# Moving three PSUM tiles of a recurrence: scores and gate product to the other pool, turned sample rows into the outputs' bank

## The chip, the core and the metric

The kernel runs on one core of a Trainium2 chip. The metric is the device time of one execution in microseconds (us), given as the median of several runs. The profile is of one execution of its own. The engines go by short names: PE is TensorE (matrix products), DVE is VectorE, ACT is ScalarE, POOL is GpSimd, SP is SyncE. PSUM is the memory that PE writes its products to and that the other engines read; it is handed out in banks, and every tile of 128 x 512 float32 here is one bank.

## What is computed

One layer of a decoder step for 256 prompt rows and 8 x 8 sample rows (T = 320 columns in the kernel, the first TP = 256 of them the prompt): norm, one wide projection, three branches, an output projection and a gated feed-forward part. The change lies in the first branch, a recurrence over tokens with a 64 x 64 state for each of 12 heads:

```python
def _wkv7_step(S, inp):
    r, w, k, v, kk, a = inp
    sa = jnp.einsum('bhvk,bhk->bhv', S, -kk)
    S = S * w[:, :, None, :] + sa[..., None] * (kk * a)[:, :, None, :] + v[..., None] * k[:, :, None, :]
    return S, jnp.einsum('bhvk,bhk->bhv', S, r)
...
    s_fin, o = lax.scan(_wkv7_step, s0.astype(f32), xs)
    o = jnp.swapaxes(o, 0, 1)
    mean = jnp.mean(o, axis=-1, keepdims=True)
    var = jnp.mean(jnp.square(o - mean), axis=-1, keepdims=True)
    o = (o - mean) * lax.rsqrt(var + RW_GN_EPS)
    o = o.reshape(b, t, RW_WIDTH) * prm['ln_x_w'].astype(f32) + prm['ln_x_b'].astype(f32)
    bonus = jnp.sum(r * k * prm['r_k'].astype(f32), axis=-1, keepdims=True) * v
    o = (o + bonus.reshape(b, t, RW_WIDTH)) * g.astype(f32)
```

The prompt starts from a state of zeros; the sample rows start from eight given states, one for each group of eight rows.

## The kernel before

**Fill.** All large projections are a queue of jobs. A step of a job multiplies a 128 x 128 piece of weights with 320 columns; the product is made of three passes (lines 102 to 104), of the weights' high and low part (`wh`, `wl`) with the activations' high and low part. ScalarE rounds a loaded piece to `wh` (line 374) and VectorE subtracts for `wl` (line 375), a few pieces ahead. While the recurrence runs, these jobs fill PE between its steps.

**The recurrence** takes the heads in six pairs, called pairs 1 to 6 here. For each pair three generators run: `early` (lines 509 to 631), `inverse` (633 to 675) and `late` (677 to 797). A program-building loop (`pump`) advances a clock by a constant for every step of fill and resumes a generator when the time that its last `yield` gave is over or its condition holds. So the order of PE's instructions is the order in which the code is run: PE's order is written by hand (`MANUAL` holds PE alone), and PE takes it strictly in that order. The other engines' order comes from a scheduler, which places instructions by estimates of its own; when the program is built, a changed dependency can move instructions on VectorE, ScalarE and GpSimd too.

**What one pair does, in order.** `early`: two small products for decay and rate (lines 513 to 515); element-wise work on VectorE that ends with `ar` (line 555); the scores, 20 small products in chunks of 32 rows, chunks 0 to 7 into `ps1` and 8 to 9 into `ps2` (lines 566 and 571 to 574), which VectorE masks into `BT` (line 569); the masked scores go through DRAM (lines 579 and 582) into `NI`; transposes of `bk`, `ar` and `sv` (lines 589, 595). `inverse`: a triangular inverse of `NI` by many small VectorE operations (lines 643 to 663), then the result `R` goes back through DRAM (line 666) to `IT` (line 671, four DMAs). `late`: a solve with `IT`; in the bank `pso` the product of the samples' states (line 714), which opens the bank; ScalarE copies a part of it to `Wu` (line 716). Then the carry products of the prompt's chunks (line 724), in two groups with a bank each, out of which VectorE adds `AB` and a new `ar` (lines 727 and 730); the state products into `psb` (line 734); `Wu` turned into `psu` by four products with the identity (line 739), which VectorE adds in two halves to rows of `AU` (line 743); 16 products into `pso` for the prompt's outputs (line 749); then seven hops from state to state (line 753) with fill in between; and last the rest of the outputs into `pso` (lines 758 to 765), the new sample states `pss`, the output norm, and the gate's product `psg` (line 793), which VectorE multiplies in (line 795).

**Banks.** The small tiles share two pools of two banks each, `pea` and `pch`, in which a new tile takes the bank of the tile before last and must wait until that one has been read. Before the change everything in `early` and everything from the output norm on takes from `pea`; `late` takes from `pch` through the helper `bank()`: two tiles of the solve, two of the carry, `psu`, `pss`. So `psu` gets the bank of the first group of the carry. `pso` and `psb` have a pool of one bank each, and `pso` uses columns 0 to 255 for outputs of the prompt, TP = 256 to 319 for outputs of the samples and 320 to 383 for what becomes `Wu`.

Of the kernel before, what the change touches and what calls it, by code (L numbers as in the profile page):

```python
# [9 lines left out]
F32 = mybir.dt.float32  # L10
# [6 lines left out]
T = 320  # L17
TP = 256
# [45 lines left out]
def tile_hybrid_step(ctx: ExitStack, tc: tile.TileContext, i, o):  # L64
    nc = tc.nc
    V, A, G, PE = nc.vector, nc.scalar, nc.gpsimd, nc.tensor
# [9 lines left out]
    C = {n: cst[:, s] for n, s in COFF.items()}  # L76
# [65 lines left out]
    def spread(psum, ex, nh, tbs=TB):  # L142
        ps = psum.tile([128, 512], F32, tag="sm", name="sm")
        n = 0
        for j, (_, c0, c1) in enumerate(tbs):
            lhs = ex[:, j:j + 1].to_broadcast([128, 128]) if nh == 1 else ex[:, j, :]
            PE.matmul(ps[:, n:n + c1 - c0], lhs, C["ident"][:, c0:c1], start=True, stop=True)  # L147
            n += c1 - c0
        return ps[:, :n]
# [19 lines left out]
    with tc.tile_pool(name="st", bufs=1, side="right") as st, tc.tile_pool(name="st2", bufs=3, side="right") as st2, \  # L169
# [136 lines left out]
        sm = spread(smp, smt, 1, tbs=TB[:2])  # L306
# [121 lines left out]
    with tc.tile_pool(name="rws", bufs=1, side="right") as rws, tc.tile_pool(name="rwp", bufs=2, side="right") as rwp, \  # L428
# [29 lines left out]
        Wu = rws.tile([128, TS], F32, name="Wu")  # L458
# [50 lines left out]
        def early(hp):  # L509
# [49 lines left out]
            AU = rwm.tile([128, 10, 128], F32, tag="AU", name="AU")  # L559
            AP = rwm.tile([128, 5, 128], F32, tag="AP", name="AP")  # L560
            fss = [slice(64 * h, 64 * h + 64) for h in range(2)]

            def scores(pv, lo, hi):
                for c in range(lo, hi):
                    for fs in fss:
                        PE.matmul(pv[fs, c - lo, :].rearrange("p (x t) -> p x t", x=2), bk[fs, c, :], ar[fs, :, 32 * c:32 * c + 32], start=True, stop=True)
# [1 line left out]
            def masked(pv, lo, hi, mask):  # L568
                V.tensor_mul(out=BT[:, lo:hi, 64:128], in0=pv, in1=C[mask].unsqueeze(1).to_broadcast([128, hi - lo, 64]))

            ps1 = pea.tile([128, 512], F32, tag="sm", name="sm").rearrange("p (c t) -> p c t", t=64)
            ps2 = pea.tile([128, 512], F32, tag="sm", name="sm").rearrange("p (c t) -> p c t", t=64)
            scores(ps1, 0, 8)
            scores(ps2, 8, 10)
            masked(ps1, 0, 8, "tmask")
# [10 lines left out]
            ps1 = pea.tile([128, 512], F32, tag="sm", name="sm")  # L586
            ps2 = pea.tile([128, 512], F32, tag="sm", name="sm")
# [23 lines left out]
            ps1 = pea.tile([128, 512], F32, tag="sm", name="sm")  # L611
# [7 lines left out]
            ps1 = pea.tile([128, 512], F32, tag="sm", name="sm").rearrange("p (c t) -> p c t", t=64)  # L619
# [8 lines left out]
            bonus = rwm.tile([128, T], F32, tag="bonus", name="bonus")  # L628
            V.tensor_mul(out=bonus, in0=psb, in1=sv)
            spawn(late(hp, ar, pc, bonus, BT, it, AU, AP))  # L630
            state["early"] = hp + 1

# [44 lines left out]
        def late(hp, ar, pc, bonus, BT, it, AU, AP):  # L677
# [6 lines left out]
            fss = [slice(64 * h, 64 * h + 64) for h in range(2)]  # L684
            uss = [slice(64 * h, 64 * h + 32) for h in range(2)]

            def bank():
                return pch.tile([128, 512], F32, tag="sm", name="sm")
# [12 lines left out]
            ps1, ps2 = bank(), bank()  # L701
# [8 lines left out]
            pso = psop.tile([128, 512], F32, tag="acc", name="pso")  # L710
            psw = pso[:, TP:TP + 128].rearrange("p (x t) -> p x t", x=2)
            for b in range(8):
                for fs in fss:
                    PE.matmul(psw[fs, :, 8 * b:8 * b + 8], S0[fs, b, :], ar[fs, :, TP + 8 * b:TP + 8 * b + 8],
                              start=b == 0, stop=False, skip_group_check=True)
            A.copy(out=Wu, in_=psw[:, 1, :])
            yield SLV
            for lo, hi in ((1, 5), (5, 8)):
# [6 lines left out]
                for h in range(2):  # L725
                    hs = slice(64 * h, 64 * h + 64)
                    V.tensor_add(out=AB[hs, lo - 1:lo - 1 + n, hs], in0=pv[hs, 0:n, 0:64],
                                 in1=C["ident"][hs, hs].unsqueeze(1).to_broadcast([64, n, 64]))
# [3 lines left out]
            for c in range(8):  # L732
                for h in range(2):
                    PE.matmul(psb[fss[h], 64 * c:64 * c + 64], BT[fss[h], c, 0:64], AU[fss[h], c, 64:128],
                              start=c == 0, stop=c == 7, skip_group_check=True)
            psu = bank()
            for cc in range(2):
                for h in range(2):
                    PE.matmul(psu[uss[h], 64 * cc:64 * cc + 64], Wu[fss[h], 32 * cc:32 * cc + 32], C["ident"][fss[h], fss[h]], start=True, stop=True)
            SA = rw1.tile([128, 8, 64], F32, tag="SA", name="SA")  # L740
            A.activation(out=SA[:, 0, :], in_=psb[:, 0:64], func=AF.Copy, scale=pc[:, 0:1])
            for h in range(2):
                V.tensor_add(out=AU[uss[h], 8:10, 64:128], in0=psu[uss[h], 0:128].rearrange("p (c v) -> p c v", v=64), in1=AU[uss[h], 8:10, 64:128])
            UVm = rw1.tile([128, 512], F32, tag="UVm", name="UVm").rearrange("p (c s v) -> p c s v", s=4, v=64)
            G.tensor_mul(out=UVm, in0=AU[:, 8:10, 64:128].unsqueeze(2).to_broadcast([128, 2, 4, 64]),
                         in1=C["smask"].unsqueeze(1).unsqueeze(3).to_broadcast([128, 2, 4, 64]))
            for c in range(8):
                for h in range(2):
                    PE.matmul(pso[fss[h], 32 * c:32 * c + 32], AU[fss[h], c, 64:128], BT[fss[h], c, 64:96],
                              start=False, stop=False, skip_group_check=True)  # L750
            yield HOP
            for c in range(1, 8):
                PE.matmul(psb[:, 64 * c:64 * c + 64], AB[:, c - 1, :], SA[:, c - 1, :], start=False, stop=True,
                          skip_group_check=True)
# [3 lines left out]
            for c in range(1, 8):  # L758
                for h in range(2):
                    PE.matmul(pso[fss[h], 32 * c:32 * c + 32], SA[fss[h], c - 1, :], ar[fss[h], 0, 32 * c:32 * c + 32],  # L760
                              start=False, stop=False, skip_group_check=True)
            for c in range(8, 10):
                for h in range(2):
                    PE.matmul(pso[fss[h], 32 * c:32 * c + 32], AU[fss[h], c, 64:128], BT[fss[h], c, 64:96],
                              start=False, stop=c == 9, skip_group_check=True)
# [23 lines left out]
            V.tensor_mul(out=ob, in0=ob, in1=rn)  # L789
            A.activation(out=ob, in_=ob, func=AF.Identity, scale=col("lnw", hp), bias=col("lnb", hp))  # L790
            yield 2.0
            psg = pea.tile([128, 512], F32, tag="sm", name="sm")[:, :T]
            PE.matmul(psg, lw[:, 1, cs], lora[1], start=True, stop=True)
            V.tensor_add(out=ob, in0=ob, in1=bonus)
            V.tensor_mul(out=ob, in0=psg, in1=ob)
# [3 lines left out]
        def allearly():  # L799
            for hp in range(6):  # L800
                yield from early(hp)
# [284 lines left out]
    with tc.tile_pool(name="mg", bufs=1, side="right") as mg, tc.tile_pool(name="mg2", bufs=2, side="right") as mg2, \  # L1086
# [76 lines left out]
        for k in range(16):  # L1163
            for half in range(2):
                for j in range(4):
                    h, l = wc[k // 8 * 4 + j]
# [15 lines left out]
    with tc.tile_pool(name="ff", bufs=1, side="left") as ff, tc.tile_pool(name="fft", bufs=2, side="left") as fft, \  # L1182
# [7 lines left out]
        for g, gn in enumerate((8, 8, 8, 8, 8, 4)):  # L1190
            fs = []
            for jj in range(gn):
# [7 lines left out]
                             in1=S2[:, TP:T].rearrange("p (b t) -> p b t", t=8))  # L1200
                for e in range(2):
                    G.tensor_copy(out=cout[:, j, :, e], in_=zp[:, 256 + e:337 + e:10])  # L1202
                c = fft.tile([128, 336], F32, tag="cv", name="cv")
# [9 lines left out]
                             in1=c[:, 256:336].rearrange("p (b t) -> p b t", t=10)[:, :, 2:10])  # L1213
# [27 lines left out]
        with tc.manual_schedule(engines=MANUAL):  # L1241
            for q, sq_ in enumerate((facc, sq)):
                for j, (t0, _, _) in enumerate(TB):
                    PE.matmul(pst[:, j:j + 1], sq_[:, t0:t0 + 128], C["ones"][:, 0:1], start=q + j == 0, stop=q == 1,  # L1244
                              skip_group_check=True)
                for _ in range(7):
                    PE.matmul(wps, fs[1][0][:, 0:128], fs[0][0], start=True, stop=True)  # L1247
        v = fft.tile([128, 8], F32, tag="rsv", name="rsv")[:, :3]
# [4 lines left out]
        with tc.tile_pool(name="pt", bufs=3, space=PSUM) as ptp:  # L1253
            sy = spread(smp, r, 1)
            A.copy(out=SY, in_=sy)
            for m, n, en in TAIL:
# [6 lines left out]
                t = ptp.tile([128, 2, 512], F32, tag="t", name="pt")[:, :n, :T]  # L1263
# [138 lines left out]
```

## Time and profile before

| quantity | value |
|---|---|
| median of the runs | 2039.72 us (2036.27, 2039.72, 2040.2) |
| the profiled execution | 2036.6 us |
| its span, first to last instruction | 2034.8 us |
| granted TensorE clock, mean over the span | 0.988 |
| busy share of the span: PE, DVE, ACT, POOL | 97%, 60%, 41%, 10% |
| PE's longest wait by line: line 739 for line 730 of VectorE | 17.6 us in 5 waits |

The profile is read in four steps: the busy times say which engine bounds the kernel; the list of waits says what that engine waited for, line by line; the timeline of one place says who came when, with idle time in square brackets ahead of the instruction that ended it and the instruction that released it; and the table by stretches says at which clock TensorE ran there (1.00 is 2.4 GHz, 0.50 is 1.2 GHz).

### The profile page before, as it was taken

How to read it: one execution, taken by the hardware profiler on the slowest of the kernel's cores; microseconds unless marked ns; L12 is line 12 of the kernel's file. 1: busy time of each engine (PE TensorE's matmuls, PEld its weight loads, DVE VectorE, ACT ScalarE, POOL GpSimd, SP SyncE). 2: the span in 40 equal slices, each digit the busy share in tenths (PEclk: the TensorE clock that was granted, in tenths of full speed). 3: DMA queues.
4: the chain of work that ended last, by engine and by line, in shares of the span. 5: the costliest groups of instructions: out<-in, count | busy, mean ns of one | idle time of the engine just before them, and what ended most of it. 6: DMA issues, size and time to landing. Idle time of an engine off the chain costs nothing.

```text
span 2034.8 us, 36379 instructions
## 1 busy us (share of the span) xinstructions
PE 1981.6 (97%) x14888; PEld 1928.4 (95%) x14888; DVE 1215.6 (60%) x2019; ACT 829.2 (41%) x1353; POOL 195.7 (10%) x446
## 2 busy tenths in 40 slices
PE   8999898899999999999999999999999999999997
PEld 8888898889998999999999999999999999999997
DVE  7788868874467754444447653554555555555456
ACT  5544344333444433333444433333343333343335
POOL 4412122211200000000100100000000000000001
PEclk9999899999999999999999999999999999999999
DMA  7543343333645444544552444454444444444433
GB/s 277 174 140 120 95 134 102 101 103 128 203 169 160 136 130 153 160 152 150 194 187 91 155 145 153 148 179 161 150 151 147 154 146 155 146 155 146 151 135 127
DMA packets 89688, 303.28 MB, mean 149 GB/s; under 512 B 11500, under 2 KB 13190, under 8 KB 89504
## 3 DMA queue, kind: packets, MB, share of 16 engines
q1 hardware_dynamic: 79920, 273.42, 40.1%
q0 software_dynamic: 8880, 26.71, 3.9%
q8 instruction: 117, 1.92, 0.4%
q10 hardware_dynamic: 720, 0.82, 0.1%
q14 instruction: 51, 0.42, 0.1%
HBM read 293.53 MB, written 9.34 MB: 149 GB/s over the span
## 4 chain that ended last, share of the span: by engine, by line
PE 57%; issue 5%; POOL 1%; DVE 0%; ACT 0%; POOLq 0%; DVEq 0%
PE bigps L102 18%; PE bigps L103 18%; PE bigps L104 18%; PE bigps L1171 0%; PE bigps L1169 0%; PE bigps L1172 0%; POOL merged L1094 0%; POOL yacc L1259 0%; POOL yacc L1260 0%; DVE MG L845 0%; PE sm L147 0%; POOL rsr L1119 0%; PE sm L1244 0%; PE sm L1112 0%; PE sm L1247 0%
## 5 line engine op out<-in xcount | busy, mean ns | idle before, releaser
L102 PE MATMUL bigps<-XH,wh 128*128 128x320 f32 x2656 | 843.7, 318 | 0.9 <-ACT gt L862 0.8
L104 PE MATMUL bigps<-XH,wl 128*128 128x320 f32 x2656 | 824.0, 310 | 1.4 <-DVE wl L375 1.3
L103 PE MATMUL bigps<-XL,wh 128*128 128x320 f32 x2656 | 823.7, 310 | 0.0
L98 DVE TENSOR_TENSOR wl<-raw,wh 128x1024 fp32r<-128x1024 f32 (+1 forms) x299 | 357.5, 1195 | 275.3 <-ACT wh L97 274.7
L97 ACT CAST wh<-raw 128x1024 fp32r<-128x1024 f32 (+1 forms) x299 | 306.5, 1025 | 521.5 <-PE bigps L103 412.8
L102 PEld LDWEIGHTS bigps<-XH,wh 128*128 128x128 f32 x2656 | 501.6, 189 | 14.1 <-issue 8.6
L103 PEld LDWEIGHTS bigps<-XL,wh 128*128 128x128 f32 x2656 | 501.9, 189 | 2.2 <-issue 0.2
L104 PEld LDWEIGHTS bigps<-XH,wl 128*128 128x128 f32 x2656 | 501.3, 189 | 2.4 <-DVE wl L375 2.4
L375 DVE TENSOR_TENSOR wl<-raw,wh 128x1024 fp32r<-128x1024 f32 (+2 forms) x212 | 243.2, 1151 | 184.5 <-ACT wh L374 182.0
L374 ACT CAST wh<-raw 128x1024 fp32r<-128x1024 f32 (+2 forms) x212 | 208.4, 984 | 313.0 <-PE bigps L103 250.9
L103 PE MATMUL bigps<-fl,wh 128*128 128x320 f32 x704 | 217.5, 309 | 0.0
L102 PE MATMUL bigps<-fh,wh 128*128 128x320 f32 x704 | 217.4, 309 | 0.0
L104 PE MATMUL bigps<-fh,wl 128*128 128x320 f32 x704 | 217.4, 309 | 0.0
L102 PEld LDWEIGHTS bigps<-fh,wh 128*128 128x128 f32 x704 | 132.2, 188 | 0.2 <-ACT fh L152 0.2
L103 PEld LDWEIGHTS bigps<-fl,wh 128*128 128x128 f32 x704 | 132.2, 188 | 0.1
L104 PEld LDWEIGHTS bigps<-fh,wl 128*128 128x128 f32 x704 | 132.2, 188 | 0.0
L1228 DVE TENSOR_TENSOR yacc<-yacc,bigps 128x320 f32<-128x320 f32 x80 | 38.9, 487 | 84.4 <-PE bigps L104 84.4
L1202 POOL COPY cout<-zp 128x9 f32<-128x9 f32 x88 | 15.5, 206 | 734.0 <-DVE zp L1199 734.0
L102 PE MATMUL bigps<-MG,wh 128*128 128x320 f32 x208 | 64.4, 309 | 0.3 <-ACT MG L844 0.3
L103 PE MATMUL bigps<-MG,wh 128*128 128x320 f32 x208 | 64.3, 309 | 0.0
L104 PE MATMUL bigps<-MG,wl 128*128 128x320 f32 x208 | 64.3, 309 | 0.0
L1198 DVE TENSOR_TENSOR zp<-bigps,S 128x256 f32<-128x256 f32 x44 | 18.7, 425 | 57.0 <-PE bigps L104 57.0
(407 smaller groups left out, 2358.4 us busy)
## 6 DMA issues: line engine op xcount, KB each, us to landing
raw<-in_wup SPq DMA_DIRECT2D x176, 512.0 KB, 3.5
raw<-in_win SPq DMA_DIRECT2D x164, 512.0 KB, 3.6
raw<-in_wdn SPq DMA_DIRECT2D x80, 512.0 KB, 3.2
raw<-in_wo SPq DMA_DIRECT2D x32, 512.0 KB, 3.7
raw<-in_wbr_rw SPq DMA_DIRECT2D x16, 384.0 KB, 3.2
raw<-in_wbr_sw SPq DMA_DIRECT2D x16, 384.0 KB, 3.1
ck<-in_cmk POOLq DMA_DIRECT2D x8, 512.0 KB, 5.1
cv<-in_cmv POOLq DMA_DIRECT2D x8, 512.0 KB, 4.2
```

Of the source, the lines that this page charges most:

```text
L97: A.copy(out=h, in_=raw)
L98: V.tensor_sub(out=l, in0=raw, in1=h.bitcast(F32))
L102: PE.matmul(ps, h, xh, start=start, stop=False)
L103: PE.matmul(ps, h, xl, start=False, stop=False)
L104: PE.matmul(ps, l, xh, start=False, stop=stop)
L374: A.copy(out=h, in_=c[2])
L375: V.tensor_sub(out=l, in0=c[2], in1=h.bitcast(F32))
L1198: V.tensor_mul(out=zp[:, 2:258], in0=psz[:, 0:TP], in1=S2[:, 0:TP])
L1202: G.tensor_copy(out=cout[:, j, :, e], in_=zp[:, 256 + e:337 + e:10])
L1228: V.tensor_add(out=yacc[:, m, :], in0=yacc[:, m, :], in1=ps)
```

## The change

Three tiles get another place in PSUM. The computation is the same.

- The two tiles of the scores (`ps1`, `ps2`) come from `pch` instead of `pea`.
- The gate's product `psg` comes from `pch` (through `bank()`) instead of `pea`.
- `psu`, the turned sample rows, no longer gets a bank of its own from `bank()`. It lies in columns TP + 128 to TP + 255 of `pso` (384 to 511), which nothing used. Since the bank was opened by line 714, its products go without the start flag.

```diff
--- before.py
+++ after.py
@@ -568,8 +568,8 @@
             def masked(pv, lo, hi, mask):
                 V.tensor_mul(out=BT[:, lo:hi, 64:128], in0=pv, in1=C[mask].unsqueeze(1).to_broadcast([128, hi - lo, 64]))
 
-            ps1 = pea.tile([128, 512], F32, tag="sm", name="sm").rearrange("p (c t) -> p c t", t=64)
-            ps2 = pea.tile([128, 512], F32, tag="sm", name="sm").rearrange("p (c t) -> p c t", t=64)
+            ps1 = pch.tile([128, 512], F32, tag="sm", name="sm").rearrange("p (c t) -> p c t", t=64)
+            ps2 = pch.tile([128, 512], F32, tag="sm", name="sm").rearrange("p (c t) -> p c t", t=64)
             scores(ps1, 0, 8)
             scores(ps2, 8, 10)
             masked(ps1, 0, 8, "tmask")
@@ -733,14 +733,15 @@
                 for h in range(2):
                     PE.matmul(psb[fss[h], 64 * c:64 * c + 64], BT[fss[h], c, 0:64], AU[fss[h], c, 64:128],
                               start=c == 0, stop=c == 7, skip_group_check=True)
-            psu = bank()
+            psu = pso[:, TP + 128:TP + 256]
             for cc in range(2):
                 for h in range(2):
-                    PE.matmul(psu[uss[h], 64 * cc:64 * cc + 64], Wu[fss[h], 32 * cc:32 * cc + 32], C["ident"][fss[h], fss[h]], start=True, stop=True)
+                    PE.matmul(psu[uss[h], 64 * cc:64 * cc + 64], Wu[fss[h], 32 * cc:32 * cc + 32], C["ident"][fss[h], fss[h]],
+                              start=False, stop=True, skip_group_check=True)
             SA = rw1.tile([128, 8, 64], F32, tag="SA", name="SA")
             A.activation(out=SA[:, 0, :], in_=psb[:, 0:64], func=AF.Copy, scale=pc[:, 0:1])
             for h in range(2):
-                V.tensor_add(out=AU[uss[h], 8:10, 64:128], in0=psu[uss[h], 0:128].rearrange("p (c v) -> p c v", v=64), in1=AU[uss[h], 8:10, 64:128])
+                V.tensor_add(out=AU[uss[h], 8:10, 64:128], in0=psu[uss[h], :].rearrange("p (c v) -> p c v", v=64), in1=AU[uss[h], 8:10, 64:128])
             UVm = rw1.tile([128, 512], F32, tag="UVm", name="UVm").rearrange("p (c s v) -> p c s v", s=4, v=64)
             G.tensor_mul(out=UVm, in0=AU[:, 8:10, 64:128].unsqueeze(2).to_broadcast([128, 2, 4, 64]),
                          in1=C["smask"].unsqueeze(1).unsqueeze(3).to_broadcast([128, 2, 4, 64]))
@@ -789,7 +790,7 @@
             V.tensor_mul(out=ob, in0=ob, in1=rn)
             A.activation(out=ob, in_=ob, func=AF.Identity, scale=col("lnw", hp), bias=col("lnb", hp))
             yield 2.0
-            psg = pea.tile([128, 512], F32, tag="sm", name="sm")[:, :T]
+            psg = bank()[:, :T]
             PE.matmul(psg, lw[:, 1, cs], lora[1], start=True, stop=True)
             V.tensor_add(out=ob, in0=ob, in1=bonus)
             V.tensor_mul(out=ob, in0=psg, in1=ob)
```

Lines from 740 on are one further down in the changed kernel: line 743 becomes 744, 749 becomes 750, 793 becomes 794, 795 becomes 796.

On PE, in pair 1, from the second group of the carry products (into the bank `sm`) to the end of the outputs' products into `pso`; in brackets the engines whose counts an instruction waits for. Before:

```order
L724 MATMUL sm<-BT,AU 64x96 [waits PE_49]
L724 MATMUL sm<-BT,AU 64x96 x5
L734 MATMUL psb<-AU,BT 64x64 x16
L739 MATMUL sm<-cst,Wu 32x64 [waits DVE_49,PE_49,Activation_49]
L739 MATMUL sm<-cst,Wu 32x64 x3
L749 MATMUL pso<-BT,AU 64x32 x16
```

After:

```order
L724 MATMUL sm<-BT,AU 64x96 [waits PE_49]
L724 MATMUL sm<-BT,AU 64x96 x5
L734 MATMUL psb<-AU,BT 64x64 x16
L739 MATMUL pso<-cst,Wu 32x64 [waits Activation_49]
L739 MATMUL pso<-cst,Wu 32x64 x3
L750 MATMUL pso<-BT,AU 64x32 [waits DVE_49]
L750 MATMUL pso<-BT,AU 64x32 x15
```

The order of the products is the same; the wait on VectorE moved from line 739 to the first product of line 750, and the count that it waits for is the one that the second addition of line 744 brings. The other five pairs read the same way.

On GpSimd, behind the end of pair 1 (`S` are the sample states, `sc` the tile in DRAM between lines 666 and 671, `rsr` a reciprocal root of the output norm, `pc` decay factors for the next pair but one; the numbers count tiles). Before:

```order
L773 DMA out_wkvs<-S_1389 128x512
L666 DMA sc_2523<-R 120x192
L474 COPY shout<-pad 128x9
L681 DMA S_2208<-in_wkv 128x512
L469 MEMSET pad 128x1
L470 COPY pad<-shs 128x8
L671 DMA IT_775<-sc_2523 32x5x32 x3
L136 TENSOR_TENSOR rsr<-rsv,mhalf 128x6
L537 COPY pc<-rt 128x8
L538 COPY pc<-rt 128x8
L671 DMA IT_775<-sc_2523 32x5x32
```

After:

```order
L666 DMA sc_2522<-R 120x192
L774 DMA out_wkvs<-S_1389 128x512
L671 DMA IT_775<-sc_2522 32x5x32
L474 COPY shout<-pad 128x9
L671 DMA IT_775<-sc_2522 32x5x32
L681 DMA S_2207<-in_wkv 128x512
L469 MEMSET pad 128x1
L470 COPY pad<-shs 128x8
L671 DMA IT_775<-sc_2522 32x5x32 x2
L537 COPY pc<-rt 128x8
L538 COPY pc<-rt 128x8
L136 TENSOR_TENSOR rsr<-rsv,mhalf 128x6
```

The reciprocal root (line 136) moved behind all four DMAs of line 671 and behind lines 537 and 538, and the first DMA of line 671 moved to two places behind line 666.

## Rows read from the trace of the kernel before

**Rows 1.** The page, section 1: busy time, share of the span, instructions.

```profile
PE 1981.6 (97%) x14888; PEld 1928.4 (95%) x14888; DVE 1215.6 (60%) x2019; ACT 829.2 (41%) x1353; POOL 195.7 (10%) x446
```

**Rows 2.** Waits of PE: us in total, number of waits, longest.

```profile
PE sm L739 <- DVE ar L730: 17.6, 5, 4.6
PE sm L566 <- DVE ar L555: 3.2, 2, 1.8
PE sm L793 <- DVE rp L789: 2.2, 2, 1.9
PE sm L566 <- DVE rp L795: 1.8, 2, 1.2
```

**Rows 3.** Timeline of pair 2: start, length, instruction, [idle before, releaser].

```profile
244.64 0.29 DVE L730 TENSOR_TENSOR ar<-sm,ar 128x128 f32<-128x128 f32 x1
...
245.08 0.64 PE L739 MATMUL sm<-cst,Wu 64*32 64x64 f32 x8 [4.04 <-DVE ar L730]
...
245.65 1.92 PE L749 MATMUL pso<-BT,AU 64*64 64x32 f32 x32
...
245.77 0.57 DVE L743 TENSOR_TENSOR AU<-sm,AU 32x128 f32<-32x128 f32 x2
```

**Rows 4.** Stretches: length, PE, PEld, DVE, ACT, POOL busy, PEclk, DMA, GB/s.

```profile
100.20:103.60 3.40, 3.39 (x54) 3.32 (x55) 3.40 (x5) 0.00 (x0) 1.15 (x1) 1.00 0.37 87
207.10:210.50 3.40, 3.40 (x14) 3.22 (x14) 3.40 (x8) 0.11 (x2) 2.27 (x2) 0.50 0.00 0
244.60:251.40 6.80, 6.32 (x55) 6.11 (x56) 6.03 (x12) 0.41 (x2) 1.04 (x1) 0.50 0.01 2
```

**Rows 5.** Timeline of pair 1, the same place.

```profile
172.01 0.41 PE L739 MATMUL sm<-cst,Wu 64*32 64x64 f32 x8 [0.92 <-DVE ar L730]
...
172.35 1.12 PE L749 MATMUL pso<-BT,AU 64*64 64x32 f32 x32
...
172.68 0.57 DVE L743 TENSOR_TENSOR AU<-sm,AU 32x128 f32<-32x128 f32 x2
```

**Rows 6.** Timeline of pair 6, the same place.

```profile
502.33 1.12 PE L749 MATMUL pso<-BT,AU 64*64 64x32 f32 x32
...
503.66 0.59 DVE L743 TENSOR_TENSOR AU<-sm,AU 32x128 f32<-32x128 f32 x2
```

**Rows 7.** Timeline from pair 1's gate product to pair 3's scores.

```profile
206.54 0.95 PE L793 MATMUL sm<-lora,lw 128*128 128x320 f32 x2 [1.95 <-DVE rp L789]
...
211.54 1.23 DVE L375 TENSOR_TENSOR wl<-raw,wh 128x1024 fp32r<-128x1024 f32 x1 [0.87 <-ACT wh L374]
...
212.69 0.48 DVE L795 TENSOR_TENSOR rp<-sm,rp 128x320 f32<-128x320 f32 x1
...
213.23 0.45 PE L566 MATMUL sm<-ar,bk 64*64 64x64 f32 x8 [0.62 <-DVE rp L795]
```

**Rows 8.** Timeline of pair 5's scores and pair 3's gate product.

```profile
344.62 0.45 PE L566 MATMUL sm<-ar,bk 64*64 64x64 f32 x8 [0.84 <-DVE rp L789]
...
345.62 0.88 DVE L569 TENSOR_TENSOR BT<-sm,cst 128x512 f32<-128x512 f32 x2
...
346.42 0.75 PE L793 MATMUL sm<-lora,lw 128*128 128x320 f32 x2
```

**Rows 9.** Stretch of pair 3's inverse; columns as in rows 4.

```profile
224.40:244.90 20.50, 16.64 (x225) 14.53 (x223) 19.64 (x40) 7.19 (x16) 0.00 (x0) 0.99 0.40 121
```

**Rows 10.** Timeline of GpSimd behind pair 1.

```profile
194.92 0.55 POOL L666 DMA_DIRECT2D sc<-R  x1 [0.76 <-DVE R L663]
...
197.84 1.73 POOL L671 DMA_DIRECT2D IT<-sc  x3 [0.36 <-issue]
199.59 1.36 POOL L136 TENSOR_TENSOR rsr<-rsv,mhalf 128x6 f32<-128x6 f32 x1
...
201.34 0.63 POOL L671 DMA_DIRECT2D IT<-sc  x1
```

**Rows 11.** DMA issues: queue, number, KB each, median us to landing.

```profile
sc<-R POOLq DMA_DIRECT2D x6, 90.0 KB, 2.1
```

## The prediction, made before the changed kernel ran

> **What bounds the kernel now.** I read the page's busy times first: TensorE (PE) is busy for 97% of the span and no other engine comes near [rows 1]. So the end is moved only by what PE waits for, and by the clock it runs at. The second view is therefore the list of whom PE waited for [rows 2]. Its largest entry is the one that this change is about: the turned sample rows (line 739) waited 17.6 us, five times, for VectorE's line 730. Lines 566 (scores) and 793 (the gate's product) follow with waits for VectorE of a few us in all. Each of these is a wait for a bank: `bank()` hands line 739 the bank of the first carry product, which line 730 has to read first. The third view is the timeline at one such place, pair 2 of the heads [rows 3]: line 730 ends at 244.93 (244.64 + 0.29), line 739 starts 0.15 later after 4.04 us idle, line 749 starts at 245.65, and while line 749 writes `pso`, line 743 reads `psu` from 245.77 to 246.34. The fourth view is the granted clock [rows 4]: after that idle time TensorE runs at its lower level, 1.2 instead of 2.4 GHz (0.50), from 244.6 to 251.4, so an idle gap costs more than its length.
>
> **What the change does to line 739's wait.** It removes it: `psu` no longer needs the carry's bank, and the eight passes of line 739 can run as soon as line 734 has ended. It adds another. `psu` now lies in `pso`, and the order shown above has a new wait on VectorE at the first matmul of line 749 (750 after the change), for the count that the second addition of line 743 (744) brings. So PE now stands behind the whole of VectorE's stretch (the rest of line 727, the second line 730, both additions), which before ran beside it. VectorE's own order up to that addition is the same, so I take its times from before. Behind the waiting instruction on PE stand the other products into `pso`, then the projections of the fill, and all else.
>
> Pair 2: the second addition ends at 246.34; with the 0.15 us that the same hand-over took before, line 749 starts at 246.49 instead of 245.65: 0.84 us later, although line 739 has already run. In other words 1.41 us of VectorE (244.93 to 246.34) stand against 0.57 us of line 739 that are done earlier. Pairs 3, 4 and 5 have the same chain behind their waits, with the same instructions: 0.84 each. Pair 1 [rows 5]: 172.68 + 0.57 + 0.15 = 173.40 instead of 172.35: 1.05. Pair 6 did not wait at all, but there VectorE splits a piece of weights (line 375, 1.22 us) ahead of the addition [rows 6]: 503.66 + 0.59 + 0.15 = 504.40 instead of 502.33: 2.07. Sum: 1.05 + 4 x 0.84 + 2.07 = **+6.5 us**.
>
> Row and rule, on this point: in [rows 3] the reads of line 743 and the writes of line 749 run at the same time, in two banks; nothing in the trace has them in one. The Trainium skill, page "PSUM — Partial Sum Buffer", section "PSUM bank collisions raise a hardware error", says that PSUM has to be guarded by bank and quadrant (32 partitions) and not by address, since two engines may not touch the same bank and quadrant at once, even at different columns. By that rule the new wait is no accident of how the program was built. By quadrants alone the first product would need only the first addition, some 0.28 us less at each pair, 1.7 us less in all; the program waits for both.
>
> **What the scores and the gate's product bring.** The wait of 1.95 us at line 793 goes, since its bank now comes from the other pool [rows 7]. But scores and product now meet in that pool: at pairs 3 and 4 the second half of the scores still waits for line 795, which reads the product. VectorE goes through its list in order, and line 795 only comes at 212.69, after a split (line 375) that itself waited 0.87 us for ScalarE, which waited for PE to give a weight buffer back. With PE 1.95 us earlier these 0.87 us go; the rest of the list is VectorE's own work. So 1.95 us at one place become a longer wait at the next, and **-0.87 us** remain. At pair 4 the wait of 1.2 us for line 795 [rows 2] stays, since VectorE has no gap there; only the 0.3 us that line 793 waited (2.2 - 1.95, rounded) move into it. At pair 5 [rows 8] the scores' 0.84 us go, but the product then arrives at 345.58 and needs line 569's first half, which ends at about 346.30: the same 0.8 us one place further on. I put both at nothing.
>
> What comes after these places? The scores feed the solve's chain: its input lands by DMA at 224.4, and from there to the end of line 730 of pair 2, at 244.9, VectorE is busy for 19.64 of 20.5 us [rows 9]. So a delay at one pair passes to the next one whole, and at the end into a stretch without waits. Nothing swallows it.
>
> **The other queues.** SyncE's order is unchanged. On VectorE some splits of weights (line 375, 1.2 us each) move back by two or three instructions; further products of the fill stand between them and the products that use them, so I cost that at nothing; without this cover it would be the length of those instructions, up to 3 us of PE. On GpSimd the order moves after pair 1: the reciprocal root (line 136), for which VectorE and PE wait, started at 199.59 right behind three of the DMAs of line 671 [rows 10]. Now four of these, the first of which waits for the store of line 666 to land (2.1 us [rows 11]), the small instructions that stood between lines 666 and 671 (195.47 to 197.84, 2.37 us with their gaps) and lines 537 and 538 (between 200.95 and 201.34, 0.4) stand ahead of it. 194.92 + 2.1 + 4 x 0.58 + 2.37 + 0.4 = 202.1: 2.5 us later than before, of which 1.05 are pair 1's delay anyway. Bounds of the rest: 0 (the small instructions run while the store lands, and who waits for line 136 has that much to spare) and 1.5; I take **+1.0**, nearer to the sum.
>
> **The clock.** At pairs 2 to 5 the idle time was 3.5 to 4.6 us and the low level followed each time; about a microsecond more of idle time moves it, and I count the delay in full. If the low stretch ended at the same point as before, half of each 0.84 would be lost work instead: the lower bound, -1.7 us. New are idle gaps of 1.9 us (pair 1: 0.92 + 1.05 - 0.07) and 2.0 us (pair 6). Their nearest rows are two of the same length [rows 4]: after 1.95 us at 206.54 the level was low for 3.4 us, which costs 1.7; after 1.8 us at 100.20 (the longest wait of line 566 for line 555 [rows 2]) it stayed full. So 0 to 1.7 each, and I take 0.7 each, a chance of four in ten: **+1.4**.
>
> Sum: 6.5 - 0.9 + 1.0 + 1.4 = **+8.0 us**. The profiled execution took 2036.6 us (span 2034.8), so it would be 2044.6; that execution lies 3.1 us below the median of the runs, 2039.72, and against the median I forecast **2047.7 us**.
>
> **The rivals.**
> (a) Faster: the new wait never binds, since the additions are done by the time that PE gets to line 749. Then the 17.6 us of line 739 go, and with them four low stretches of 6.8 us, in which half is lost: up to 17.6 + 4 x 3.4 - about 6 counted twice = 25 us, 2014. It decides at 246.34: VectorE would have to end there before PE is through line 739, at about 241.5. VectorE works almost without a gap from 224.4 on, so I see nothing that speaks for it but that the wait removed is the largest. Chance 0.07.
> (b) No change: half of the four 0.84 us, no low level after the two new gaps, GpSimd in time: 1.05 + 4 x 0.42 + 2.07 - 0.87 = +3.9, 2043.6. Nothing excludes any of the three; together they are less likely. Chance 0.18.
> (c) Slower still: both new gaps are followed by the low level (+3.4), and so is the longer wait ahead of the scores of pair 3, 2 to 3 us instead of 0.62, which costs 1.7 more by the same row. 6.5 - 0.9 + 1.0 + 2 x 1.7 + 1.7 = +12, and +16 with two or three more such stretches at pairs 3 to 5: 2052 to 2056. Chance 0.14.
> The forecast, with +5 to +11, has 0.61.
>
> **How the numbers follow.** What a measurement of this kernel can tell from no change is about 0.2%, 4.1 us. Slower by more: the forecast and (c), 0.61 + 0.14 = 0.75, less a hundredth or two for its near edge: 0.74. Same: (b), 0.18. Faster: (a) and what I don't see, 0.08. The range runs from 2040.5, through (b), to 2056, the end of (c); (a) and about a tenth at both edges are left out.
>
> **What would show it.** In the list of PE's waits line 739 should be gone and line 750 stand in its place, waiting for line 744, six times, with more than 17.6 us (by the sum: 17.6 + 6.5, less the passes of line 739 now done ahead, and so 20 to 27). Line 794 should have lost its 1.95 us and the second half of line 566 at about 213 should wait 2 to 3 us for line 796. Line 136 of GpSimd should start about 2 us later. After pair 6, at 504, there is a gap of 2 us that was not there. I am wrong if line 750 starts before the additions of line 744 have ended, or if GpSimd or VectorE, off this path, shorten the way from one pair to the next by more than a microsecond.

## The result and the profile after

The changed kernel takes 2050.34 us (median; 2048.67 to 2051.38), the kernel before 2037.99 us beside it (2035.86 to 2040.2): 1.0056 times as long, 95% interval 1.0042 to 1.0071. By that ratio it is 11.4 us more (8.6 to 14.5), where +8.0 was forecast; 2050.34 lies inside the stated range. The profiled execution took 2050.13 us, its span is 2048.3 us, 13.5 more than before.

The page's busy times, section 1 (against [rows 1]):

```profile
PE 1987.1 (97%) x14888; PEld 1934.4 (94%) x14888; DVE 1214.3 (59%) x2019; ACT 829.3 (40%) x1353; POOL 199.0 (10%) x446
```

PE has the same 14888 products and is busy for 5.5 us longer: the same work at a lower clock for part of the time. The other 8 us of the span are idle time. The list of PE's waits (us in total, number, longest; against [rows 2]):

```profile
PE pso L750 <- DVE AU L744: 24.4, 6, 5.7
PE sm L566 <- DVE rp L796: 4.1, 2, 2.4
PE sm L566 <- DVE ar L555: 3.6, 3, 1.7
...
PE sm L794 <- DVE BT L569: 0.8, 1, 0.8
```

Line 739 is gone from the list. Line 750 stands in its place, six times, waiting for the additions of line 744, with 24.4 us instead of 17.6. Pair 2, in the timeline (start, length, instruction, [idle before, releaser]; against [rows 3]):

```profile
246.29 0.41 PE L739 MATMUL pso<-cst,Wu 64*32 64x64 f32 x8
...
250.31 0.29 DVE L730 TENSOR_TENSOR ar<-sm,ar 128x128 f32<-128x128 f32 x1
250.52 0.71 DVE L727 TENSOR_TENSOR AB<-sm,cst 64x192 f32<-64x192 f32 x2
251.25 0.26 DVE L730 TENSOR_TENSOR ar<-sm,ar 128x96 f32<-128x96 f32 x1
251.42 0.57 DVE L744 TENSOR_TENSOR AU<-pso,AU 32x128 f32<-32x128 f32 x2
...
252.05 0.75 PE L750 MATMUL pso<-BT,AU 64*64 64x32 f32 x10 [5.35 <-DVE AU L744]
```

Line 739 runs without a wait and is done at 246.70. Then PE stands for 5.35 us until VectorE has been through both lines 730, the rest of line 727 and the additions. From the end of the first line 730 (250.60) to the start of line 750 it takes 1.45 us; before, line 749 started 0.72 us after that end. The granted clock (length, busy times of PE, PEld, DVE, ACT, POOL, PEclk, DMA share, GB/s), at pair 1, behind line 794 (793 before, the low stretch at 207 in [rows 4]), behind the second half of pair 3's scores, and at pair 6:

```profile
174.40:184.30 9.90, 9.81 (x96) 8.86 (x96) 7.74 (x13) 1.78 (x3) 1.66 (x1) 0.51 0.01 2
209.60:213.00 3.40, 3.34 (x22) 2.91 (x20) 3.40 (x10) 1.86 (x3) 0.72 (x2) 1.00 0.12 49
218.60:221.50 2.90, 2.90 (x13) 2.86 (x13) 0.00 (x0) 0.00 (x0) 1.07 (x2) 0.50 0.43 151
...
514.90:518.60 3.70, 3.70 (x29) 3.66 (x26) 0.00 (x0) 0.18 (x1) 0.50 (x1) 0.55 0.37 134
```

and the kernel before at pair 1:

```profile
171.90:181.80 9.90, 9.79 (x131) 9.25 (x132) 9.56 (x17) 3.30 (x6) 1.70 (x1) 1.00 0.13 34
```

Behind the new gap of pair 1 TensorE runs for nearly all of 9.9 us at 1.2 GHz (0.51), where it ran at 2.4 GHz before. The low stretch behind line 793 is gone, one behind the scores has come (from 218.6; they started at 217), and pair 6 has a new one.

To see where the time goes, I took the same instruction in both traces and followed how much later it starts. Ahead of pair 1: 0.9 us. Over the wait of line 749 (750), beyond the delay that was there: 1.24, 1.09, -0.06, 1.02, 0.73 and 1.95 us at pairs 1 to 6, 6.0 in all. In the stretch just behind it: 4.3 us at pair 1, 0.6 at pair 2, 1.05 at pair 5, 1.5 at pair 6. Between pairs 1 and 2 the delay falls from 6.4 to 1.5, since the wait of line 793 and the low stretch behind it are missing here, and rises to 5.3 again. From pair 6 to the end of the recurrence it is 13.4, and it stays there.

### The profile page after: what moved, and what is told of

Its sections match the earlier page's. It is cut to its first block, busy times and chain, and to the rows that moved or that the text cites. A ratio compares the mean times of both kernels' runs of the same rounds, so it can differ in the third digit from the quotient of the medians.

```text
span 2048.3 us, 36375 instructions
## 1 busy us (share of the span) xinstructions
PE 1987.1 (97%) x14888; PEld 1934.4 (94%) x14888; DVE 1214.3 (59%) x2019; ACT 829.3 (40%) x1353; POOL 199.0 (10%) x446
## 4 chain that ended last, share of the span: by engine, by line
PE 57%; issue 5%; POOL 1%; DVE 0%; ACT 0%; POOLq 0%; ACTq 0%; DVEq 0%
PE bigps L102 18%; PE bigps L104 18%; PE bigps L103 18%; PE bigps L1172 0%; PE bigps L1170 0%; PE bigps L1173 0%; POOL yacc L1260 0%; POOL merged L1095 0%; POOL yacc L1261 0%; DVE MG L846 0%; PE sm L147 0%; POOL rsr L1120 0%; PE sm L1245 0%; PE sm L1113 0%; PE sm L1248 0%
```

## The experiments

Ratios are against the kernel before on the same chip (median 2040.4 to 2040.6 in the three sets), with 95% intervals.

| run | what it is | median us | ratio |
|---|---|---|---|
| e0_change_again | the change, once more | 2052.61 | 1.0056 (1.0044 to 1.0068) |
| e1_psu_only | only psu into the outputs' bank | 2048.52 | 1.0041 (1.0028 to 1.0053) |
| e2_pools_only | only scores and gate product | 2041.56 | 1.0005 (0.9997 to 1.0014) |
| e4_pair6 | psu in the outputs' bank at pair 6 alone | 2045.83 | 1.0023 (1.0013 to 1.0032) |
| e5_pair1 | the same at pair 1 alone | 2042.63 | 1.0008 (0.9999 to 1.0017) |
| e7_psu_early | the change, psu ahead of the carry | 2033.39 | 0.9964 (0.9951 to 0.9977) |
| e3_psu_behind | the change, psu behind the outputs' products | 2030.92 | 0.9951 (0.9938 to 0.9965) |
| f3_behind_oldpools | as e3, with the old pools | 2029.0 | 0.9940 (0.9928 to 0.9952) |
| g1_hop1_24 | as f3, 2.4 us of fill ahead of the first hop | 2029.1 | 0.9943 (0.9930 to 0.9956) |
| g2_hop1_48 | as f3, 4.8 us of it | 2028.4 | 0.9942 (0.9930 to 0.9954) |
| g3_before_fill | before, 4.0 us of fill ahead of psu | 2028.27 | 0.9942 (0.9930 to 0.9954) |
| e6_fill_between | the change, 2.4 us of fill ahead of line 750 | 2023.9 | 0.9922 (0.9909 to 0.9935) |

**Which part of the change costs.** The two parts were run apart. First psu alone:

```diff
-            psu = bank()
+            psu = pso[:, TP + 128:TP + 256]
...
-                    PE.matmul(psu[...], Wu[...], C["ident"][...], start=True, stop=True)
+                    PE.matmul(psu[...], Wu[...], C["ident"][...], start=False, stop=True, skip_group_check=True)
```

> Only the turned sample rows move into the outputs' bank; scores and gate product stay where they were. Theory A (the bank shared by psu and pso makes PE stand behind VectorE's additions, and low clock follows the two new gaps at pairs 1 and 6): most of the loss is here, +9 to +13 us against before, six waits of line 749 for line 743 with 22 to 26 us in all, and the low clock after pair 1 as in the changed kernel. Theory B (the scores meeting the gate's product in one pool is what costs): only +3 to +6 us.

It took 0.41% more, 8.4 us, just under the band of theory A and above that of B; theory A's six waits and its low stretch behind pair 1 are there (1.2 GHz from 176.3 on, for 6.8 us). Its list of waits has the new entry and keeps the old one of line 793:

```profile
PE pso L749 <- DVE AU L743: 24.4, 6, 5.8
...
PE sm L793 <- DVE rp L789: 2.2, 2, 1.9
```

Then the pools alone (the two lines of `ps1` and `ps2` and the one of `psg` from the change):

> Only scores and gate product change pools; psu keeps a bank of its own as before. Theory A: -2 to +1 us: the 1.95 us of line 793 (794) and the low clock behind it go, and a wait of about 2.4 us of the scores of pair 3 for line 795 (796) with 1.7 us of low clock comes. Theory B: +5 us or more, since the scores wait for the product at several pairs.

It took 0.05% more, 1.0 us (-0.6 to 2.9): no difference that these runs can tell, and far from theory B. Here the order on VectorE, ScalarE and GpSimd is that of the kernel before, so the trace shows the pools by themselves:

```profile
205.38 0.70 PE L793 MATMUL sm<-lora,lw 128*128 128x320 f32 x2
...
209.69 1.15 PE L566 MATMUL sm<-ar,bk 64*64 64x64 f32 x32 [0.97 <-DVE ar L555]
...
211.54 1.23 DVE L375 TENSOR_TENSOR wl<-raw,wh 128x1024 fp32r<-128x1024 f32 x1
212.68 0.49 DVE L795 TENSOR_TENSOR rp<-sm,rp 128x320 f32<-128x320 f32 x1
213.23 0.69 PE L566 MATMUL sm<-ar,bk 64*64 64x64 f32 x8 [2.39 <-DVE rp L795]
```

```profile
211.60:218.50 6.90, 5.27 (x26) 5.12 (x27) 2.79 (x6) 0.46 (x1) 1.21 (x2) 0.51 0.57 164
```

The gate's product no longer waits and starts 1.2 us earlier. The scores then wait 0.97 us for line 555 and 2.39 for line 795, which starts at the same time as before (212.68, against 212.69 in [rows 7]). That is a gain: up to this place PE and VectorE are 0.9 us late in this trace (a difference between executions that stands in it since 135, and in that of pair 6 alone too), and the split (line 375) at 211.54 makes it good, since it no longer waits the 0.87 us of [rows 7]. But the clock is low from 211.6 to 218.5, twice as long as behind line 793 before, and line 589 is 2.3 us later than before. So the loss is psu's, and the two parts together, 8.4 + 1.0, lie within the interval of the whole.

**How much of it is the gap and how much the clock.** At pair 6 PE had no wait before and nothing of the recurrence follows; at pair 1 there was a short one. Each was changed alone (the start flag goes with it; `hp == 0` for pair 1):

```diff
-            psu = bank()
+            psu = pso[:, TP + 128:TP + 256] if hp == 5 else bank()[:, 0:128]
```

> The kernel before, with psu in the outputs' bank at pair 6 alone, where PE did not wait before and nothing of the recurrence follows. Theory A with the clock at its low level behind the gap, as the trace of the changed kernel shows it: +1.9 for the gap and +1.5 for the clock, +3.4 us. As the prediction sized it: 2.07 + 0.7 = +2.8 us. Rival (something later takes the delay up): 0.

> The kernel before, with psu in the outputs' bank at pair 1 alone. Theory A: the gap grows from 0.92 to about 2.1 us and a low stretch of 7 to 10 us follows, which was not there before: 1.3 + 3.5 to 4.5 us behind pair 1; of that some 1 to 2 us are given back before pair 2, so +3 to +5 us at the end. As the prediction sized it: 1.05 + 0.7 = +1.8 us. Rival (the order of the other engines, which moves too, is the cause): the drift begins ahead of pair 1's line 739 and no low stretch follows it.

Pair 6 alone costs 0.23%, 4.7 us (2.7 to 6.5). Its trace, the same place and then the stretch behind it:

```profile
504.60 1.22 DVE L375 TENSOR_TENSOR wl<-raw,wh 128x1024 fp32r<-128x1024 f32 x1
505.73 0.57 DVE L743 TENSOR_TENSOR AU<-pso,AU 32x128 f32<-32x128 f32 x2
506.35 1.91 PE L749 MATMUL pso<-BT,AU 64*64 64x32 f32 x32 [1.87 <-DVE AU L743]
```

```profile
506.40:513.90 7.50, 7.50 (x56) 7.43 (x57) 0.00 (x0) 0.41 (x2) 1.05 (x1) 0.54 0.23 72
```

The gap is 1.87 us, as in the changed kernel, but the low stretch behind it is about twice as long: some 6.9 us here (0.54 over 7.5 us) and 3.3 there (0.55 over 3.7). By the same instructions in both traces the gap costs 1.94 us and the clock 3.1; nothing gives it back, so the rival, 0, falls. The interval holds both the forecast's 2.8 and the 3.4 of theory A, so the time alone doesn't decide between them; the trace shows the stretch. VectorE, ScalarE and GpSimd take their instructions in this run in the order of the kernel before, so the bank of this one tile is all that differs.

Pair 1 alone costs 0.08%, 1.6 us (-0.2 to 3.5), less than theory A's 3 to 5 and at the forecast's 1.8. Its trace has the low stretch all the same:

```profile
175.90:182.50 6.60, 6.60 (x82) 5.64 (x83) 4.89 (x9) 0.42 (x1) 1.66 (x1) 0.50 0.01 2
```

The delay against before is 2.53 us ahead of pair 1, grows by 0.95 over the gap and by 3.05 behind it, and falls by 1.7 up to line 589 at 220, so 2.3 us remain of pair 1's own. In the run with psu alone it is 2.3 as well (2.18 ahead of pair 1, 4.47 at line 589). So the low stretch behind pair 1 is real, and over 40% of the loss is swallowed before pair 3's transposes, since PE waits for VectorE in between anyway, and waits less when it arrives later. The rival of this run, the order of the other engines, falls: the 2.53 us are there before line 749, but a low stretch follows it, and the order differs only behind that line.

**Is the low stretch an accident?** The changed kernel was run again:

> The changed kernel as it is, on the same chip as the runs of this call, to see how much its low-clock stretches differ from one execution to the next. Theory A (the stretch behind a gap is either there or not and begins at the gap, but its length differs between executions): +8 to +14 us against before, the same six waits of line 750 with 23 to 26 us, and the low stretch behind pair 1's gap is there again, 3 to 11 us long. If it were an accident of one execution: no low stretch behind pair 1, and +5 to +8 us.

1.0056 again. The waits are the same, and so are the places of the low clock:

```profile
PE pso L750 <- DVE AU L744: 24.7, 6, 5.8
```

```profile
175.30:182.30 7.00, 7.00 (x68) 6.07 (x65) 6.16 (x10) 1.30 (x3) 0.90 (x1) 0.53 0.01 2
517.00:520.00 3.00, 3.00 (x12) 3.00 (x13) 0.00 (x0) 0.09 (x1) 0.00 (x0) 0.50 0.39 150
```

At pair 1 the stretch is 7 us instead of 9.9. Over the traces of the change (two), of psu alone, of pair 6 alone and of pair 1 alone there are eight gaps of 1.87 to 2.15 us ahead of line 749 or 750 at pairs 1 and 6, and a low stretch comes with each of them. Its length, 3 to 10 us, is not set by the gap. At other places gaps of this length did not always bring one; the last section counts them.

**Is it the shared bank or PE's place in line?** The bank stays shared, but the additions come elsewhere. Behind the outputs' products, PE needs nothing from them for a long time:

```diff
-            psu = pso[:, TP + 128:TP + 256]
-            ... (its four products, the two additions, UVm)
             for c in range(8):
                 for h in range(2):
                     PE.matmul(pso[fss[h], 32 * c:32 * c + 32], AU[fss[h], c, 64:128], BT[fss[h], c, 64:96], ...)
+            psu = pso[:, TP + 128:TP + 256]
+            ... (its four products, the two additions, UVm)
             yield HOP
```

> The changed kernel, with the four products of psu and the two additions put behind the 16 outputs' products into pso, so that nothing that PE does next needs the additions. Theory A: the six waits (24.4 us) and the low clock behind them (about 3.5 us at each of pairs 1 to 5, 1.5 at pair 6) go: 2010 to 2030 us. Rival C (VectorE's list paces each pair, so PE only arrives earlier at its next wait for VectorE): the waits come back at the solve, the scores and the carry products, and the time is 2034 to 2045 us.

Ahead of the carry products, VectorE adds before it reads the carry:

> The changed kernel with the products of psu and both additions ahead of the carry products, so that VectorE adds them before it reads the carry; the bank is shared as in the change. Theory A (PE stands behind the whole stretch of VectorE from line 727 to the second addition): line 749 then waits only for additions that end about 2.0 us sooner, so 24.4 - 6 x 2.0 = about 12 us of waits and 8 to 14 us less than the changed kernel: 2036 to 2043 us. Theory B (sharing the bank costs by itself, wherever the additions stand): no better than the changed kernel, 2048 to 2052.

With a piece of fill between psu and line 750, all else as in the change:

```diff
+            yield 2.4
             for c in range(8):
                 for h in range(2):
                     PE.matmul(pso[fss[h], 32 * c:32 * c + 32], AU[fss[h], c, 64:128], BT[fss[h], c, 64:96], ...)
```

> The changed kernel with 2.4 us of fill put between the products of psu and the first product of line 750; bank, pool and wait stay as in the change. Theory A (what costs is only that PE stands at the new wait with nothing to do): 24.4 us of waits become 10 to 13, and low clock behind pairs 1 and 6 goes: 8 to 16 us less than the changed kernel, 2035 to 2043 us. Rival (the fill is only taken from a later place, where the wait opens again): 2046 to 2053 us.

All three are faster than the kernel before: by 0.49%, 0.36% and 0.78%. Theory B of the second, that sharing the bank costs by itself, falls. Psu behind came out at 2030.92, just above the band of theory A and under that of rival C; what holds it back is shown further below. Psu early, whose line 749 waits for line 723 (the additions):

```profile
PE pso L749 <- DVE AU L723: 10.9, 5, 3.4
```

That is the 24.4 less some 2.2 us a pair, as theory A had it; the time came out 3 us under the band, since low stretches go too. With the fill between, the fastest of all (there the additions are line 743 and the hops line 754):

```profile
PE psb L754 <- ACT SA L756: 7.0, 3, 3.3
PE pso L750 <- DVE AU L743: 6.3, 4, 2.4
...
PE sm L147 <- DVE rex L139: 4.0, 2, 2.5
```

```profile
core 0: 2021.3 us, clock 0.994
```

The same wait at the same bank is down to 6.3 us, and the mean clock is 0.994 instead of 0.984. Theory A had this run at 2035 to 2043; it came out at 2023.9. Of the wait 18.1 us are gone, and of PE's busy time 16.5 (1970.6 us against 1987.1, for the same products), while 7.0 us of new waits at the hops and 4.0 at line 147 stand against it: 23.6 of the 27.0 us between the two spans (all idle time together is 10.5 us less). What theory A missed are the low stretches of pairs 2 to 5, which mostly went as well. Pairs 1, 3, 4 and 6 have no low stretch there; the 7 us behind pair 1:

```profile
172.00:179.00 7.00, 7.00 (x119) 6.17 (x116) 6.70 (x16) 1.79 (x3) 1.72 (x1) 1.00 0.19 65
```

**Why psu behind the products gains no more.** With psu behind the outputs' products the 24.4 us of waits are gone, and the span is 2026.4 us, 21.9 less than the change's though low clock went too. The list shows what came instead:

```profile
PE psb L753 <- ACT SA L755: 4.9, 2, 3.2
PE sm L566 <- DVE rp L795: 4.8, 2, 2.4
PE psb L753 <- DVE AB L727: 4.2, 3, 1.8
```

PE now reaches the hops (line 753) before `AB` and `SA` are there. The wait of 3.18 us at pair 3:

```profile
314.25 0.33 PE L753 MATMUL psb<-SA,AB 128*128 128x64 f32 x2
...
318.41 0.47 ACT L531 ACTIVATE rt<-rt 128x320 f32<-128x320 f32 x1 [4.99 <-DVE rt L522]
318.79 0.30 ACT L755 ACTIVATE SA<-psb,pc 128x64 f32<-128x64 f32 x1
...
319.14 0.47 PE L753 MATMUL psb<-SA,AB 128*128 128x64 f32 x2 [3.18 <-ACT SA L755]
```

The hop's product is done at 314.6, but ScalarE takes its list in order, and line 531 stands ahead of line 755 and waits 4.99 us for VectorE. The old pools should take away the wait for line 795, and more fill ahead of the first hop the waits for `AB`:

```diff
             (psu behind the outputs' products, scores and gate product from pea as before)
-            yield HOP
+            yield 2.4
             for c in range(1, 8):
                 PE.matmul(psb[:, 64 * c:64 * c + 64], AB[:, c - 1, :], SA[:, c - 1, :], ...)
```

> The products of psu behind the outputs' products as in the experiment that was faster, but scores and gate product in the pool that they had before. Theory A (the pools are worth nothing either way): 2028 to 2033 us. Theory D (with PE earlier the scores meet the gate's product in one pool for longer, 4.8 us of waits, and the old pools avoid it): 2024 to 2028 us.

> The fastest version so far (psu behind the outputs' products, old pools, 2029.0 us), with 2.4 instead of 1.2 us of fill ahead of the first hop, where PE now waits 4.0 us for AB (line 727) and 4.9 for SA. Theory A: half of these waits go and the time is 2023 to 2028. Rival C (VectorE's list paces the pair): 2028 to 2033.

> As the run before, with 4.8 us of fill ahead of the first hop. Theory A: the waits of the hops are gone and the time is 2020 to 2027. Rival C: the fill is missing further on, and the time is 2030 to 2038.

The old pools give 2029.0 (0.9940 against 0.9951: the intervals overlap, so theory A of that run stands and D isn't shown). The fill ahead of the first hop gives nothing more: 2029.1 and 2028.4, so theory A of these two runs falls. In the second the waits for `AB` are gone, but the wait for `SA` has become larger. What ScalarE did ahead of the two longest, at pairs 3 and 4:

```profile
PE psb L753 <- ACT SA L755: 11.8, 4, 5.1
```

```profile
312.74 0.47 ACT L531 ACTIVATE rt<-rt 128x320 f32<-128x320 f32 x1 [7.27 <-DVE rt L522]
...
383.81 0.56 ACT L527 ACTIVATE rt<-rkv,prm 128x320 f32<-128x320 f32 x1 [5.20 <-DVE rkv L478]
```

So it is ScalarE's list that paces the hops once PE is early: lines 531 and 527, which wait for VectorE, stand in it ahead of line 755. That is near rival C, by way of ScalarE, though the second time, 2028.4, lies under C's band. I did not move these lines, so whether that would free the hops stays open.

**Was the change needed at all for the gain?** The kernel before, with fill ahead of its old wait:

```diff
+            yield 4.0
             psu = bank()
```

> The kernel before, pools and banks as they were, with 4.0 us of fill ahead of line 739, which waited 17.6 us for line 730. Theory A (only PE's place in line counts, not the bank): the five waits shrink to 1 to 5 us in all, and with them the low-clock stretches: 2024 to 2033 us. Rival C (the wait only moves on to the hops and the solve): 2036 to 2043 us.

2028.27 us, 0.9942: the wait of line 739 for line 730 has left the list, and the hops (line 754 there) wait instead:

```profile
PE psb L754 <- ACT SA L756: 11.5, 7, 5.1
```

Pools and banks are those of before. So most of the gain comes from fill at this place and not from a bank; the version with the shared bank and 2.4 us of fill was 0.2% faster than this one on the same chip, 2023.9 against 2028.27, with intervals (0.9909 to 0.9935, 0.9930 to 0.9954) that just overlap, though no run of the one (up to 2025.85) is as slow as the fastest of the other (2026.6). The two differ in the amount of fill and in its place as well as in the bank and the pools, so that difference can't be put down to the bank.

## Why the prediction was right, and where it was off

- **The new wait** is where the prediction put it: line 750 for line 744, six times, 24.4 us (20 to 27 were named). The sum of the delays over it is 6.0 us in the trace against 6.5; pair 1 is 1.24 (1.05), pair 6 1.95 (2.07), pairs 2 to 5 together 2.8 (3.4). At pair 3 there was none, where the chain passed no more delay than PE had anyway. Rival (a), that the wait never binds, fell at all six pairs.
- **The clock** is the term that was mis-sized. 0.7 us each was taken for the new gaps at pairs 1 and 6, a chance of four in ten. The low level came with all eight such gaps that were traced at these two places; it cost 4.3 and 1.5 us in the profiled execution, 3.1 and 1.5 in the repeat, 3.1 at pair 6 alone. The bound of 1.7 was half of one row's stretch (3.4 us), taken as if every stretch were that long, though the same rows had one of 6.8 at 244.6. And the chance of four in ten came from two rows; the trace of before held another, a gap of 1.36 us ahead of line 130 with a low stretch behind it:

```profile
405.00:408.40 3.40, 3.40 (x46) 3.00 (x44) 1.71 (x3) 0.00 (x0) 2.27 (x1) 0.51 0.68 196
```

  The low level behind both gaps is rival (c)'s mechanism, and the measured +11.4 lies between the forecast's +5 to +11 and the +12 to +16 of (c).
- **"Nothing swallows it"** failed at pair 1: of the 4.0 us that pair 1 alone loses there, 1.7 are back at line 589 of pair 3, since PE has waits for VectorE in between. Two misses of opposite sign so met at this pair, and its net 2.3 us is near the forecast's 1.75.
- **The pools** were taken at -0.87 us and measured at +1.0 (-0.6 to 2.9). What the waits bring was right: the wait moved from line 793 to line 566, 2.39 us at 217 (2 to 3 were named), the split's 0.87 us went in the run of the pools alone, and at pair 5 the 0.8 us moved to line 794. The low stretch behind the scores, which rival (c) had and the forecast put at nothing, costs 2.3 us there and eats the gain. (The prediction also calls all the waits of line 566 waits for a bank; those for line 555 are for the operand `ar`, and no pool moves them.)
- **GpSimd** was taken at +1.0 and cost nothing. Line 136 started 4.35 us later than before, but PE was already 5.9 us late at that point, and line 147 at 206.7 didn't wait for it:

```profile
200.44 0.59 POOL L671 DMA_DIRECT2D IT<-sc  x1 [1.55 <-DMA sc<-R]
...
203.94 1.70 POOL L136 TENSOR_TENSOR rsr<-rsv,mhalf 128x6 f32<-128x6 f32 x1
```

  The wait for the store came as foreseen (1.55 us). What was missed is that line 136 may be late by as much as PE is.
- **The first 0.9 us**, ahead of pair 1, are no part of the change: PE waits 1.76 us for a split (line 375) at 134.7, against 0.91 before, and in the runs of the pools alone and of pair 6 alone, whose order on VectorE is that of before, it is 1.57 and 1.78. Executions differ by that much.
- **The rule on PSUM** was weighed as no number of the sum. In every trace here that shares the bank no product of PE into `pso` starts while VectorE or ScalarE reads it, as the Trainium skill ("PSUM — Partial Sum Buffer", section "PSUM bank collisions raise a hardware error") wants it; what two engines in one bank at once would do, no run here shows.

So the prediction was right in sign, place and cause; its size was 3.4 us short by the ratio. In the profiled pair, without the first 0.9 us, the terms are: the waits 6.0 us (6.5 forecast), the clock at pairs 1 and 6 5.8 (1.4), the clock behind pairs 2 and 5 another 1.65 (nothing), and 1.1 given back between pairs 1 and 2, where pools and GpSimd together had +0.1. The misses have both signs, so that the total came nearer than the clock's term is in part luck.

## What to carry to other kernels

To give a tile a place in a bank that is already in use takes away the wait for a bank of its own, but every later write to that bank then stands behind the tile's readers, as line 750 did here; look at what the engine does next, and put work that doesn't touch the bank between the tile's products and the next write. An idle gap on TensorE should be priced with the low-clock stretch behind it, which cost 1.5 to 4.3 us at pairs 1 and 6, where gaps had grown by 1 to 2, and with a chance, since not every gap brings one. Where an engine waits in a hand-written order, try filler at that place before a new layout: here the filler alone (0.9942) gave as much as the best rearrangement without it (0.9940).

## What was not expected of the hardware

Gaps of 1.87 to 2.15 us ahead of line 749 or 750 at pairs 1 and 6 brought TensorE to 1.2 GHz, eight times out of eight. But a gap's length alone doesn't tell. In the stretch from 90 to 560 us the traces of all runs hold ten more gaps of this length; with seven a low stretch begins by 4 us behind the gap's end, with three none does. One of the three is pair 5 in the run with psu early, ahead of the same products; and in the run with the fill between a gap of 3.34 us is not followed by one either. Each gap's row, and the stretch behind it:

```profile
442.60 0.60 PE L749 MATMUL pso<-BT,AU 64*64 64x32 f32 x14 [1.97 <-DVE AU L723]
442.60:446.60 4.00, 4.00 (x52) 3.96 (x53) 3.88 (x9) 1.59 (x3) 1.04 (x1) 1.00 0.04 13
...
385.58 0.43 PE L754 MATMUL psb<-SA,AB 128*128 128x64 f32 x2 [3.34 <-ACT SA L756]
385.60:389.60 4.00, 4.00 (x44) 3.93 (x44) 0.40 (x2) 2.14 (x6) 2.32 (x4) 1.00 0.61 161
```

What decides it, these runs don't show. The length differs too: behind gaps of 1.87 us at pair 6 the clock stayed low for some 3.3 us in one execution and 6.9 in another, and at pairs 2 to 5 for 6.8 to 10 us in runs whose code at that place is the same:

```profile
245.60:252.40 6.80, 4.71 (x48) 4.50 (x49) 6.55 (x14) 0.67 (x2) 1.05 (x1) 0.51 0.16 58
311.00:321.00 10.00, 7.37 (x59) 6.84 (x61) 7.91 (x15) 1.59 (x3) 1.59 (x1) 0.51 0.16 54
```

(pairs 2 and 3 of the run with the pools alone.) The spread among the runs of one kernel, 2035 to 2045 us before, goes in part with the clock: over the 49 runs of the kernel before in the three sets, those with a mean granted clock of 0.985 took 2042.5 us on average, those with 0.989 took 2039.1 (correlation of time and clock -0.65).
